# SSD decay factors: cumulative sums repeated over partitions from DRAM with a mask by GpSimd, instead of selector and mask matmuls

## The chip, the cores and the metric

The kernel runs on one core of a Trainium2 chip. The metric is the device time of one execution in microseconds (us). The engines are PE (TensorE, matmuls), DVE (VectorE) and ACT (ScalarE, elementwise work), POOL (GpSimd) and SP (which here issues DMAs). Each works through its own list of instructions in order; semaphores tie the lists together, so an instruction whose input isn't there holds up everything behind it on its engine.

## The reference

A trunk of two layers over 512 tokens of width 1024. Each layer is half a SwiGLU feed-forward block, a mixer, and another half block. The mixer of layer 0 is SSD (a selective state-space scan), that of layer 1 is S5. The change lies in SSD, whose scan goes over chunks of Q = 128 tokens; `bsz` is 1, there are 8 groups of 4 heads of 64 channels, with a state of 128:

```python
def step(state, inp):
    xc, dtc, bc, cc = inp
    cs = jnp.cumsum(dtc * A, axis=1)
    seg = cs[:, :, None] - cs[:, None]
    decay = jnp.exp(jnp.where(causal[None, :, :, None, None], seg, -jnp.inf))
    cb = jnp.einsum('btgn,bsgn->btsg', cc, bc)
    dtx = dtc[..., None] * xc
    y_diag = jnp.einsum('btsgk,bsgkp->btgkp', cb[..., None] * decay, dtx)
    y_off = jnp.einsum('btgn,bgkpn->btgkp', cc, state) * jnp.exp(cs)[..., None]
    to_end = jnp.exp(cs[:, -1:] - cs)
    new_state = (state * jnp.exp(cs[:, -1])[..., None, None]
                 + jnp.einsum('bsgn,bsgkp->bgkpn', bc, to_end[..., None] * dtx))
    return new_state, y_diag + y_off
```

Around it, `xs`, `bm` and `cm` come from projections of the normalised input, each followed by a causal convolution over 4 tokens and a silu; `z` comes from two gate projections for each group; the scan's output is gated by silu(z), normalised for each group and projected back.

## The kernel before

The stages follow each other: feed-forward (f1 of layer 0), SSD, f2, f1 of layer 1, S5, f2. Activations lie with channels on partitions and the 512 tokens along the row. Weights come by SP DMAs in blocks of 128 columns (`wst`, 4 buffers), are split into a rounded part `whi` (ACT, L213, 3 buffers) and a remainder `wlo` (DVE, L215), and a projection (`proj`, L222 to L224) is 24 matmuls of 128x512: high by high, low by high, high by low, for 8 blocks of the input.

In the SSD stage `dt` is projected first, `cs` (the cumulative sum, heads on partitions, tokens along the row) is made from it, and then the loop over groups g runs six projections: B, C, xs0, xs1 (each with `conv`: product with the input's scale L356, L358 and three L360, then `silu` L366), gate0 and gate1 (L390, L392). Between them, `pop()` sets in pieces of the scan of the group before, in this order: after B `states` and `decay(0)`, after C `outp(0)` and `decay(1)`, after xs0 `outp(1)`, after gate0 `norm`. After gate1 comes `head` of the group itself (L404 C by B into PSUM, copied by ACT as `cb` in L406; transposes of xs, L413, whose products with `dt` are L418; transposes of B, L424) and `final` of the group before (L160 spreads the group norm `nw_y` over partitions). For the first group, `head` stands behind the next group's B and every piece is one place later. After group 4 the first half of the output projection is made (8 blocks of 24 matmuls), with the pieces of scan 4 between them; at the end stand blocks of 12 matmuls, with the pieces of scan 7 between them.

`decay(e)` makes for the two heads h of half e the matrix of factors from token s (partition) to token t (row): PE copies row h of `cs` onto all partitions with a selector of ones (L454; `cshl` is `cs` split into two rounded parts), adds -1e30 above the diagonal (L455), ACT takes the exponential with -cs(s) as the bias (L459), and DVE multiplies by `cb` (L460). `outp(e)` likewise spreads `cs` over 64 partitions a head (L471) and takes its exponential (L473) as the factor of the state's part.

PE's order is the order of the program. The order on DVE, ACT, POOL and SP is set by a scheduler when the kernel is built. PSUM has two pools of 4 banks: `mm` for projections (and L471), `aux` for the rest: `head` takes four of `aux` for C by B, twice xs and B, so that L160 behind it takes the first again.

Of the kernel before, what the change touches and what calls it, by code (L numbers as in the profile page):

```python
# [30 lines left out]
def trunk_kernel(ctx, tc, x, ffn1_norm, ffn1_w_in, ffn1_w_out, mix_norm, ffn2_norm, ffn2_w_in, ffn2_w_out,  # L31
# [26 lines left out]

    ident = const.tile([128, 128], F32, name="ident")
    make_identity(nc, ident)  # L60
    identr = const.tile([128, 128], F32R, name="identr")
    ones = const.tile([128, 128], F32, name="ones")
    V.memset(ones, 1.0)
    kmask = const.tile([128, 16], F32, name="kmask")
# [2 lines left out]

    def masks():

        V.tensor_copy(identr, ident)  # L70
        V.tensor_reduce(kmask, ident.rearrange("p (k q) -> p k q", q=8), axis=AX.X, op=OP.add)
        V.tensor_reduce(qres, ident.rearrange("p (k q) -> p q k", q=8), axis=AX.X, op=OP.add)
        V.tensor_copy(qsel.rearrange("p (c q) -> p c q", q=8), qres[:, None, :].to_broadcast([128, 16, 8]))
# [51 lines left out]
    def both(*fs):  # L125
        return lambda: [f() for f in fs]
# [142 lines left out]
    def ssd(pr, nxt):  # L269
        w_in, w_out = ssd_in_proj[0], ssd_out_proj[0]  # L270
        with ExitStack() as es:
            sc = es.enter_context(tc.tile_pool(name="ssdc", bufs=1))
            sp = es.enter_context(tc.tile_pool(name="ssd", bufs=2))

            wd = wpool.tile([128, KD, 128], F32, name="wst", bufs=4)
            nc.sync.dma_start(wd[:, :, 0:32], w_in[:, 6144:6176].rearrange("(k p) c -> p k c", p=128))
            for q in range(1, 4):
# [3 lines left out]
            v = sp.tile([128, T], F32, name="y")  # L281
            V.tensor_tensor(v, pd, pr.rbc, op=OP.mult)
            V.tensor_scalar(v, v, col("dtb"), None, op0=OP.add)
            ax = sp.tile([128, T], F32, name="m")
            V.scalar_tensor_tensor(ax, v, -1.0, v, op0=OP.mult, op1=OP.max)
            ex = sp.tile([128, T], F32, name="m")
            S.activation(ex, ax, AF.Exp, scale=-1.0)
            w1 = sp.tile([128, T], F32, name="cv")
            V.tensor_scalar(w1, ex, 1.0, None, op0=OP.add)
            ln = sp.tile([128, T], F32, name="y")  # L290
            S.activation(ln, w1, AF.Ln)
            rw = sp.tile([128, T], F32, name="m")
            S.activation(rw, ln, AF.Exp, scale=-1.0)
            V.scalar_tensor_tensor(w1, w1, -1.0, ex, op0=OP.add, op1=OP.subtract)
            V.tensor_tensor(w1, w1, rw, op=OP.mult)
            dt = sp.tile([128, T], F32, name="m")
            V.scalar_tensor_tensor(dt, v, 0.0, ln, op0=OP.max, op1=OP.add)
            V.tensor_tensor(dt, dt, w1, op=OP.subtract)
            acol = sc.tile([128, 1], F32, name="acol")
# [12 lines left out]
            for c in range(4):  # L312
# [1 line left out]
                             bias=cse[:, c:c + 1])  # L314
            dce = sc.tile([128, 4], F32, name="dce")
            S.activation(dce, cse, AF.Exp)
            pack = sp.tile([128, T], F32, name="m")
            V.tensor_copy(pack[0:32], dt[0:32])
            V.tensor_scalar(pack[32:64], cs[32:64], -1.0, None, op0=OP.mult)
            V.tensor_tensor(pack[64:128], dt[64:128], ew[64:128], op=OP.mult)  # L320
            tok = sc.tile([128, 4, 128], F32, name="tok")
            cshl = sc.tile([128, T], F32R, name="cshl")
            S.copy(cshl, cs)
            V.tensor_tensor(cshl[32:64], cs[32:64], cshl[32:64].bitcast(F32), op=OP.subtract)
            sel = sc.tile([128, 32], F32R, name="sel")
            V.memset(sel.bitcast(F32), 0.0)
            V.tensor_copy(sel[0:32], ident[0:32, 0:32])
            V.tensor_copy(sel[32:64], ident[32:64, 32:64])
            mneg = sc.tile([128, 128], F32R, name="mneg")
            mf = sp.tile([128, 128], F32, name="mf", bufs=1)  # L330
            G.memset(mf, 0.0)
            G.affine_select(out=mf, in_=mf, compare_op=OP.is_ge, fill=-1e30, base=0, pattern=[[1, 128]],
                            channel_multiplier=-1)
            V.tensor_copy(mneg, mf)
# [60 lines left out]
            def scan(g, BT, CT, XS, SZ):  # L395
# [33 lines left out]
                def states():  # L429
# [15 lines left out]
                        SS[c + 1] = sn  # L445
                    st["SS"] = SS

                def decay(e):

                    M = []  # L450
                    for hh in range(2):
                        h = 4 * g + 2 * e + hh
                        pE = aux_ps()
                        PE.matmul(pE, sel[:, h:h + 1].to_broadcast([128, 128]), cshl, start=True, stop=False)  # L454
                        PE.matmul(pE, identr, mneg[:, None, :].to_broadcast([128, 4, 128]), start=False, stop=True)  # L455
                        m = sp.tile([128, T], F32, name="m")
                        for c in range(4):
                            s = slice(c * 128, (c + 1) * 128)
                            S.activation(m[:, s], pE[:, s], AF.Exp, bias=tok[:, c, 32 + h:33 + h])  # L459
                        V.tensor_tensor(m, m, st["cb"], op=OP.mult)  # L460
                        M.append(m)
                    st["M", e] = M

                def outp(e):
                    M = st["M", e]

                    selp = sp.tile([128, 2, 64], F32R, name="selp")
                    h0 = 4 * g + 2 * e
                    V.tensor_copy(selp, sel[:, h0:h0 + 2].bitcast(F32)[:, :, None].to_broadcast([128, 2, 64]))
                    pe_ = mm_ps()  # L470
                    PE.matmul(pe_, selp.rearrange("p a b -> p (a b)"), cshl, start=True, stop=True)  # L471
                    ecs = sp.tile([128, T], F32, name="ecs")
                    S.activation(ecs[:, 128:], pe_[:, 128:], AF.Exp)  # L473
                    po = aux_ps()
                    for c in range(1, 4):
                        s = slice(c * 128, (c + 1) * 128)
                        PE.matmul(po[:, s], st["SS"][c][:, e * 128:(e + 1) * 128], CT[:, s], start=True, stop=True)  # L477
                    V.tensor_tensor(ecs[:, 128:], ecs[:, 128:], po[:, 128:], op=OP.mult)
                    py = aux_ps()
                    for c in range(4):  # L480
                        for hh in range(2):
                            s = slice(c * 128, (c + 1) * 128)
                            k0 = (2 * e + hh) * 64
                            PE.matmul(py[hh * 64:(hh + 1) * 64, s], st["dtx"][:, c, k0:k0 + 64], M[hh][:, s], start=True,  # L484
                                      stop=True)
                    y = sp.tile([128, T], F32, name="y")
                    V.scalar_tensor_tensor(y, XS[e], col("sd", 2 * g + e), py, op0=OP.mult, op1=OP.add)
                    V.tensor_tensor(y[:, 128:], y[:, 128:], ecs[:, 128:], op=OP.add)
                    V.tensor_tensor(y, y, SZ[e], op=OP.mult)
                    sq = work.tile([128, T], F32, name="sq")  # L490
                    S.activation(sq, y, AF.Square)
                    st["y", e], st["sq", e] = y, sq
# [4 lines left out]
                def final():  # L497
                    pb = bcast_rows(st["r"])
                    for e in range(2):
# [5 lines left out]
                        V.tensor_tensor(yl, yn, yh.bitcast(F32), op=OP.subtract)  # L505
                        YH[2 * g + e], YL[2 * g + e] = yh, yl

                return both(head, *fin), [both(states, lambda: decay(0)), both(lambda: outp(0), lambda: decay(1)),
                                          lambda: outp(1), lambda: None, norm], final

            pend += [lambda: None] * 4 + [dt_tok]
# [668 lines left out]
```

## Time and profile before

| | us |
|---|---|
| median of 3 runs | 2107.82 (2107.75 to 2107.94) |
| the profiled execution | 2107.72 |
| its span | 2105.8 |

The span runs from the first to the last instruction; what lies around it is 1.92 us. PE is busy for 2054.7 us of it. The SSD stage's group loop lies about from 400 to 840 us. In the rows below a row begins with its start and its duration or its counts; "[0.80 <-DVE y L308]" is idle time before it and what ended it. Elementwise rows overlap a little at their ends with the next, and matmuls much more.

### The profile page before, as it was taken

What the parts mean: (1) busy time and instruction counts of PE and PEld (TensorE: products, weight loads), DVE (VectorE), ACT (ScalarE), POOL (GpSimd) and SP (SyncE); (2) the same over time, 40 slices, a digit from 0 to 9 for tenths busy, and PEclk for the clock granted to TensorE, in tenths of its full rate; (3) what the DMA queues carried; (4) which work ended last, traced back from release to release, by engine and by line L of the source; (5) the groups of instructions that cost most, each with busy time, mean ns of one, the idle gap of its engine ahead of it and who ended that gap; (6) DMA issues with size and microseconds to landing.
All of it is one profiled execution on the core that took longest, in us unless ns stands there. A gap on an engine that the chain in (4) does not pass through costs nothing.

```text
span 2105.8 us, 27114 instructions
## 1 busy us (share of the span) xinstructions
PE 2054.7 (98%) x10755; PEld 1691.9 (80%) x10755; DVE 1255.9 (60%) x2157; ACT 793.4 (38%) x1146; POOL 41.0 (2%) x114
## 2 busy tenths in 40 slices
PE   6999999999999999999999999999996999999997
PEld 5888888888888887887778888888886888888886
DVE  5698644687875788648864554344458555444444
ACT  4322322466663665333432333222344333222232
POOL 1000000000000000000000000000001000000000
PEclk8999999999999999999999999999997999999999
DMA  9355432322223213535553363333368233332331
GB/s 203 99 124 160 140 100 81 102 79 72 72 70 88 73 51 90 168 100 162 155 144 94 97 199 92 100 95 97 96 170 244 75 96 100 93 99 82 109 92 58
DMA packets 407630, 232.67 MB, mean 110 GB/s; under 512 B 44168, under 2 KB 395568, under 8 KB 407248
## 3 DMA queue, kind: packets, MB, share of 16 engines
q1 hardware_dynamic: 381152, 203.12, 34.1%
q10 hardware_dynamic: 22208, 13.91, 2.3%
q0 software_dynamic: 4144, 13.92, 2.0%
q8 instruction: 84, 1.38, 0.3%
q14 instruction: 42, 0.34, 0.0%
HBM read 206.21 MB, written 24.18 MB: 109 GB/s over the span
## 4 chain that ended last, share of the span: by engine, by line
PE 95%; DVE 3%; ACT 1%; DMA 1%; issue 1%; ACTq 0%; SPq 0%; DVEq 0%
PE mm L222 30%; PE mm L223 29%; PE mm L224 29%; PE aux L484 1%; PE aux L434 0%; PE aux L477 0%; PE aux L454 0%; PE aux L151 0%; PE aux L978 0%; DVE z L960 0%; PE aux L223 0%; PE aux L222 0%; PE aux L224 0%; PE aux L404 0%; PE aux L455 0%
## 5 line engine op out<-in xcount | busy, mean ns | idle before, releaser
L213 ACT CAST whi<-wst 128x1024 fp32r<-128x1024 f32 (+2 forms) x357 | 361.0, 1012 | 959.5 <-PE mm L223 660.5
L222 PE MATMUL mm<-hH,whi 128*128 128x512 f32 x1800 | 704.7, 392 | 3.2 <-DVE xT L1102 3.2
L223 PE MATMUL mm<-hL,whi 128*128 128x512 f32 x1800 | 702.8, 391 | 0.0
L224 PE MATMUL mm<-hH,wlo 128*128 128x512 f32 x1800 | 702.2, 390 | 0.0
L215 DVE TENSOR_TENSOR wlo<-wst,whi 128x1024 fp32r<-128x1024 f32 (+2 forms) x357 | 418.7, 1173 | 94.8 <-ACT whi L213 90.9
L222 PEld LDWEIGHTS mm<-hH,whi 128*128 128x128 f32 x1800 | 338.6, 188 | 75.0 <-ACT hH L1096 3.4
L224 PEld LDWEIGHTS mm<-hH,wlo 128*128 128x128 f32 x1800 | 338.6, 188 | 71.0 <-issue 0.6
L223 PEld LDWEIGHTS mm<-hL,whi 128*128 128x128 f32 x1800 | 338.6, 188 | 70.1 <-issue 0.6
L223 PE MATMUL mm<-al,whi 128*128 128x512 f32 x704 | 275.5, 392 | 0.0
L224 PE MATMUL mm<-ah,wlo 128*128 128x512 f32 x704 | 275.3, 392 | 0.0
L222 PE MATMUL mm<-ah,whi 128*128 128x512 f32 x704 | 274.7, 392 | 0.0
L248 DVE TENSOR_TENSOR up<-mm,rbc 128x512 f32<-128x512 f32 x88 | 60.7, 690 | 219.2 <-PE mm L224 219.0
L260 DVE SCALAR_TENSOR_TENSOR xT<-mm,xT 128x512 f32<-128x512 f32 x96 | 66.0, 689 | 194.7 <-PE mm L224 194.7
L223 PEld LDWEIGHTS mm<-al,whi 128*128 128x128 f32 x704 | 132.1, 188 | 29.0 <-issue 0.6
L222 PEld LDWEIGHTS mm<-ah,whi 128*128 128x128 f32 x704 | 132.1, 188 | 28.9 <-issue 0.6
L224 PEld LDWEIGHTS mm<-ah,wlo 128*128 128x128 f32 x704 | 132.1, 188 | 28.6 <-issue 0.2
L245 DVE TENSOR_TENSOR gt<-mm,rbc 128x512 f32<-128x512 f32 x88 | 60.7, 690 | 155.4 <-PE mm L224 150.3
L251 ACT CAST ah<-up 128x512 fp32r<-128x512 f32 x88 | 54.9, 623 | 60.2 <-DVE up L249 59.7
L360 DVE SCALAR_TENSOR_TENSOR cv<-raw,cols,cv 128x512 f32<-128x512 f32 x96 | 70.8, 744 | 0.7
L249 DVE TENSOR_TENSOR up<-up,gt 128x512 f32<-128x512 f32 x88 | 60.7, 690 | 11.0 <-ACT gt L246 4.4
L253 DVE TENSOR_TENSOR al<-up,ah 128x512 fp32r<-128x512 f32 x88 | 60.1, 683 | 1.2 <-ACT ah L251 1.0
L246 ACT ACTIVATE gt<-gt 128x512 f32<-128x512 f32 x88 | 55.2, 627 | 7.9 <-DMA d_P<-p_ks 4.2
(342 smaller groups left out, 1720.8 us busy)
## 6 DMA issues: line engine op xcount, KB each, us to landing
wst<-in_ffn_w_in_dram SPq DMA_DIRECT2D x176, 512.0 KB, 3.8
wst<-in_ffn_w_out_dram SPq DMA_DIRECT2D x64, 448.0 KB, 3.7
wst<-in_ssd_in_proj_dram SPq DMA_DIRECT2D x48, 512.0 KB, 3.9
wst<-in_ffn_w_out_dram SPq DMA_DIRECT2D x32, 512.0 KB, 4.0
opP<-d_P SPq DMA_DIRECT2D x16, 512.0 KB, 5.3
wst<-in_s_glu_w_dram POOLq DMA_DIRECT2D x12, 512.0 KB, 5.3
d_t<-p_cs POOLq DMA_DIRECT2D x8, 512.0 KB, 4.2
wst<-in_ssd_out_proj_dram SPq DMA_DIRECT2D x8, 512.0 KB, 4.1
```

Of the source, the lines that this page charges most:

```text
L213: S.copy(hi, st)
L215: V.tensor_tensor(lo, st, hi.bitcast(F32), op=OP.subtract)
L222: PE.matmul(ps, hi[:, k], H[k], start=first and k == 0, stop=False)
L223: PE.matmul(ps, hi[:, k], L[k], start=False, stop=False)
L224: PE.matmul(ps, lo[:, k], H[k], start=False, stop=last and k == n - 1)
L245: V.tensor_tensor(gt, pg, pr.rbc, op=OP.mult)
L246: S.activation(gt, gt, AF.Silu)
L248: V.tensor_tensor(up, pu, pr.rbc, op=OP.mult)
L249: V.tensor_tensor(up, up, gt, op=OP.mult)
L253: V.tensor_tensor(al, up, ah.bitcast(F32), op=OP.subtract)
L260: V.scalar_tensor_tensor(xT[d], po, 0.5, xT[d], op0=OP.mult, op1=OP.add)
L360: V.scalar_tensor_tensor(cv, raw[:, 1 + j:T + 1 + j], col("cw", j * 32 + ct), cv, op0=OP.mult, op1=OP.add)
```

## The change

`cs` (32 heads by 512 tokens) is stored to DRAM as `d_cs` by an SP DMA. For each half of a group, POOL's queue loads two rows of it onto all 128 partitions (`dec`, 512 KB) and columns 128 to 511 of each of the two onto 64 partitions (`ecs`, 96 KB each). POOL puts -1e30 above the diagonal of each chunk with an AFFINE_SELECT. ACT's exponentials then read and write SBUF in place, and one DVE product of 128x1024 takes the place of two of 128x512. L454, L455 and L471 are gone, and so are the copies `selp` and the set-up of selector and mask. `dec` has 2 buffers of two heads each, so a load waits until PE has read the matrices of the group before; an `ecs` load waits for DVE's sum in `outp` (L487 of the changed kernel).

```diff
-            ax = sp.tile([128, T], F32, name="m")
+            ax, ex = dec2()
...
-            cshl = sc.tile([128, T], F32R, name="cshl")
-            S.copy(cshl, cs)
-            V.tensor_tensor(cshl[32:64], cs[32:64], cshl[32:64].bitcast(F32), op=OP.subtract)
-            sel = sc.tile([128, 32], F32R, name="sel")
...
+            d_cs = dram.tile([32, T], F32, name="d_cs")
+            nc.sync.dma_start(d_cs, cs[0:32])
+
+            def cs_rows(dst, h, parts):
+                n = dst.shape[-1]
+                G.dma_start(dst, bass.AP(tensor=d_cs.tensor, offset=d_cs.offset + h * T + T - n,
+                                         ap=[[0, parts]] + [[T, k] for k in dst.shape[1:-1]] + [[1, n]]))
...
+                def rows(e):
+                    h = 4 * g + 2 * e
+                    m = sp.tile([128, 2, T], F32, name="dec")
+                    cs_rows(m, h, 128)
+                    ecs = sp.tile([128, T], F32, name="ecs")
+                    for hh in range(2):
+                        cs_rows(ecs[hh * 64:hh * 64 + 64, 128:], h + hh, 64)
+                    G.affine_select(out=m.rearrange("p h (c t) -> p (h c) t", c=4),
+                                    in_=m.rearrange("p h (c t) -> p (h c) t", c=4), compare_op=OP.is_ge, fill=-1e30,
+                                    base=0, pattern=[[0, 8], [1, 128]], channel_multiplier=-1)
+                    st["M", e], st["ecs", e] = m, ecs
+
                 def decay(e):
-                    M = []
+                    m = st["M", e]
                     for hh in range(2):
                         h = 4 * g + 2 * e + hh
-                        pE = aux_ps()
-                        PE.matmul(pE, sel[:, h:h + 1].to_broadcast([128, 128]), cshl, start=True, stop=False)
-                        PE.matmul(pE, identr, mneg[:, None, :].to_broadcast([128, 4, 128]), start=False, stop=True)
-                        m = sp.tile([128, T], F32, name="m")
                         for c in range(4):
                             s = slice(c * 128, (c + 1) * 128)
-                            S.activation(m[:, s], pE[:, s], AF.Exp, bias=tok[:, c, 32 + h:33 + h])
-                        V.tensor_tensor(m, m, st["cb"], op=OP.mult)
-                        M.append(m)
+                            S.activation(m[:, hh, s], m[:, hh, s], AF.Exp, bias=tok[:, c, 32 + h:33 + h])
+                    V.tensor_tensor(m, m, st["cb"][:, None, :].to_broadcast([128, 2, T]), op=OP.mult)
                 def outp(e):
-                    pe_ = mm_ps()
-                    PE.matmul(pe_, selp.rearrange("p a b -> p (a b)"), cshl, start=True, stop=True)
-                    ecs = sp.tile([128, T], F32, name="ecs")
-                    S.activation(ecs[:, 128:], pe_[:, 128:], AF.Exp)
+                    ecs = st["ecs", e]
+                    S.activation(ecs[:, 128:], ecs[:, 128:], AF.Exp)
...
-                return both(head, *fin), [both(states, lambda: decay(0)), both(lambda: outp(0), lambda: decay(1)),
+                rows(0)
+                return both(head, *fin, lambda: rows(1)), [both(states, lambda: decay(0)), both(lambda: outp(0), lambda: decay(1)),
```

Line numbers move a little: in the changed kernel L355 is the old L358, L357 the old L360, L363 the old silu L366, L389 the old L392, L403 the old L406, L415 the old L418, L441 the old L444, L476 the old L477; L472 is the exponential of `ecs`, L465 that of `dec`, L466 the product with `cb`, L490 the square in `outp`.

ACT's order moves in two places. The first is the first group. Before, from the cast of the first weights behind `cs` on (BT and CT are the silus of B and C, xs those of xs0 and xs1, TABLE_LOAD changes between the exponential's table and the silu's):

```order
L213 CAST whi<-wst 128x1024
L366 ACT_TABLE_LOAD
L366 ACTIVATE BT<-cv,cols_104 128x512
L366 ACTIVATE CT<-cv,cols_104 128x512
L213 CAST whi<-wst 128x1024
L358 ACTIVATE cv<-raw,cols_105 128x512 x2
L213 CAST whi<-wst 128x1024
L366 ACTIVATE xs_3479<-cv,cols_104 128x512
L366 ACTIVATE xs_3520<-cv,cols_104 128x512
```

With the change, from the first exponential of `ecs` on; behind the last of these rows come the silu of xs0, a load, seven more exponentials, a load, and the silu of xs1:

```order
L472 ACTIVATE ecs<-ecs 128x384
L363 ACT_TABLE_LOAD
L363 ACTIVATE BT<-cv,cols_103 128x512
L472 ACT_TABLE_LOAD
L472 ACTIVATE ecs<-ecs 128x384
L363 ACT_TABLE_LOAD
L363 ACTIVATE CT<-cv,cols_103 128x512
L355 ACTIVATE cv<-raw,cols_104 128x512 x2
L211 CAST whi<-wst 128x1024
L465 ACT_TABLE_LOAD
L465 ACTIVATE dec<-dec,tok 128x128 x9
L363 ACT_TABLE_LOAD
```

The exponentials of both halves stand ahead of the silus of xs0 and xs1, and those of `ecs` ahead of BT and CT, so each silu changes the table.

The second place is a group in the steady part, up to the copy `cb` of its head. Before (sq is the square of outp(1), sz the silus of the gates):

```order
L491 ACTIVATE sq<-y 128x512
L366 ACT_TABLE_LOAD
L366 ACTIVATE xs_5113<-cv,cols_104 128x512
L213 CAST whi<-wst 128x1024
L358 ACTIVATE cv<-raw,cols_105 128x512
L213 CAST whi<-wst 128x1024
L366 ACTIVATE xs_5180<-cv,cols_104 128x512
L392 ACTIVATE sz_5215<-cv 128x512
L213 CAST whi<-wst 128x1024
L392 ACTIVATE sz_5300<-cv 128x512
L406 COPY cb<-aux 128x512
```

With the change, of the same group (just ahead of these rows stand a load, an `ecs` exponential, six exponentials, an L355, two exponentials, the square of outp(1), a load and the silu of xs0):

```order
L211 CAST whi<-wst 128x1024
L465 ACT_TABLE_LOAD
L465 ACTIVATE dec<-dec,tok 128x128 x8
L472 ACTIVATE ecs<-ecs 128x384
L355 ACTIVATE cv<-raw,cols_104 128x512
L211 CAST whi<-wst 128x1024
L389 ACT_TABLE_LOAD
L389 ACTIVATE sz_5151<-cv 128x512
L363 ACTIVATE xs_5116<-cv,cols_103 128x512
L211 CAST whi<-wst 128x1024
L389 ACTIVATE sz_5236<-cv 128x512
L403 COPY cb<-aux 128x512
```

Eight exponentials, the `ecs` of the second half and two table loads have moved in ahead of `cb`; before, eight exponentials stood ahead of the group's CT and the other eight behind `cb`.

On DVE, behind the products L418 of the first group's head, from the first state on, before (L438, L440 and L444 are the states' chain, st the states):

```order
L438 COPY st_3717<-aux 128x256
L215 TENSOR_TENSOR wlo<-wst,whi 128x1024
L440 TENSOR_TENSOR st_3719<-st_3717,decS 128x256
L360 SCALAR_TENSOR_TENSOR cv<-raw,cols_105,cv 128x512
L444 TENSOR_TENSOR st_3719<-st_3719,aux 128x256
L460 TENSOR_TENSOR m<-m,cb 128x512
L360 SCALAR_TENSOR_TENSOR cv<-raw,cols_105,cv 128x512
L440 TENSOR_TENSOR st_3722<-st_3719,decS 128x256
L460 TENSOR_TENSOR m<-m,cb 128x512
L360 SCALAR_TENSOR_TENSOR cv<-raw,cols_105,cv 128x512
L444 TENSOR_TENSOR st_3722<-st_3722,aux 128x256
```

With the change, from the last two of those products on (behind these rows come an L357 and the last state's L437 and L441):

```order
L415 TENSOR_TENSOR wx<-aux,tok 128x256
L415 TENSOR_TENSOR dtx<-aux,tok 128x512
L466 TENSOR_TENSOR dec<-dec,cb 128x1024 x2
L357 SCALAR_TENSOR_TENSOR cv<-raw,cols_104,cv 128x512
L353 TENSOR_TENSOR raw<-mm,rbc 128x512
L357 SCALAR_TENSOR_TENSOR cv<-raw,cols_104,cv 128x512
L435 COPY st_3717<-aux 128x256
L213 TENSOR_TENSOR wlo<-wst,whi 128x1024
L357 SCALAR_TENSOR_TENSOR cv<-raw,cols_104,cv 128x512
L437 TENSOR_TENSOR st_3719<-st_3717,decS 128x256
L357 SCALAR_TENSOR_TENSOR cv<-raw,cols_104,cv 128x512
L441 TENSOR_TENSOR st_3719<-st_3719,aux 128x256
```

The products with `cb` stand together ahead of the chain of states, as two rows of 1024 columns; before, two of 512 columns stood within the chain.

## Rows read from the trace of the kernel before

**Rows 1.** The page's first part: busy time, share, instructions.
```profile
PE 2054.7 (98%) x10755; PEld 1691.9 (80%) x10755; DVE 1255.9 (60%) x2157; ACT 793.4 (38%) x1146; POOL 41.0 (2%) x114
```

**Rows 2.** What PE waited for, 380 to 860: total, times, longest.
```profile
PE aux L160 <- DVE nw_y L142: 0.9, 1, 0.9
PE aux L477 <- DVE st L444: 0.5, 1, 0.5
```

**Rows 3.** PE by line, 390 to 860: busy, mean ns, idle before.
```profile
L454 PE MATMUL aux<-cshl,sel 128*128 128x512 f32 x32 | 14.9, 467 | 0.0
```

**Rows 4.** Timeline of PE at the first `outp`: start, duration.
```profile
458.32 0.39 PE L471 MATMUL mm<-cshl,selp 128*128 128x512 f32 x1
458.55 0.83 PE L477 MATMUL aux<-CT,st 128*128 128x128 f32 x6
...
460.33 0.50 PE L454 MATMUL aux<-cshl,sel 128*128 128x512 f32 x1
```

**Rows 5.** Timeline of DVE around the first head.
```profile
444.14 1.23 DVE L215 TENSOR_TENSOR wlo<-wst,whi 128x1024 fp32r<-128x1024 f32 x1 [0.15 <-ACT whi L213]
445.28 0.68 DVE L418 TENSOR_TENSOR wx<-aux,tok 128x512 f32<-128x512 f32 x1
...
446.48 0.74 DVE L360 SCALAR_TENSOR_TENSOR cv<-raw,cols,cv 128x512 f32<-128x512 f32 x1
```

**Rows 6.** Timeline of ACT in a steady group.
```profile
549.82 1.28 ACT L366 ACT_TABLE_LOAD   x1
551.12 0.72 ACT L366 ACTIVATE CT<-cv,cols 128x512 f32<-128x512 f32 x1
...
554.09 0.49 ACT L473 ACTIVATE ecs<-mm 128x384 f32<-128x384 f32 x1
```

**Rows 7.** Timeline of ACT in the first group.
```profile
422.08 0.62 ACT L323 CAST cshl<-y 128x512 fp32r<-128x512 f32 x1 [0.80 <-DVE y L308]
423.28 1.28 ACT L313 ACTIVATE cv<-y,cse 128x128 f32<-128x128 f32 x4 [0.58 <-DVE cse L310]
...
426.01 1.03 ACT L213 CAST whi<-wst 128x1024 fp32r<-128x1024 f32 x1
...
438.58 1.34 ACT L366 ACTIVATE xs<-cv,cols 128x512 f32<-128x512 f32 x2
```

**Rows 8.** DMA issues of the whole span: count, size, median us to landing.
```profile
wst<-in_s_glu_w_dram POOLq DMA_DIRECT2D x12, 512.0 KB, 5.3
d_t<-p_cs POOLq DMA_DIRECT2D x8, 512.0 KB, 4.2
...
wst<-in_ssd_out_proj_dram SPq DMA_DIRECT2D x16, 256.0 KB, 2.7
```

**Rows 9.** Timeline of POOL: an issue, a mask, one copy made twice.
```profile
165.31 0.53 POOL L783 DMA_DIRECT2D d_t<-p_cs  x1 [7.23 <-DVE p_tb L561]
...
397.69 0.29 POOL L332 TENSOR_SCALAR_AFFINE_SELECT mf<-mf 128x128 f32<-128x128 f32 x1
...
1589.17 0.60 POOL L945 COPY rh<-rho 128x504 f32<-128x504 f32 x1
...
1597.67 1.08 POOL L945 COPY rh<-rho 128x504 f32<-128x504 f32 x1
```

**Rows 10.** Timeline of PE at the first head.
```profile
443.99 1.04 PE L413 MATMUL aux<-ident,xs 128*128 128x128 f32 x8
```

**Rows 11.** Timeline of all engines at a steady head.
```profile
567.01 0.15 DVE L135 TENSOR_SCALAR nw_v<-aux 128x4 f32<-128x4 f32 x1
...
569.18 1.06 PE L404 MATMUL aux<-CT,BT 128*128 128x128 f32 x8
...
569.45 0.69 DVE L390 TENSOR_TENSOR cv<-mm,rbc 128x512 f32<-128x512 f32 x1
...
570.72 0.57 ACT L406 COPY cb<-aux 128x512 f32<-128x512 f32 x1
...
571.34 0.65 PE L160 MATMUL aux<-ident,nw_y 128*128 128x128 f32 x4
```

More of the change, by code (lines that the diff above doesn't have):

```diff
@@ L60, in trunk_kernel @@
     make_identity(nc, ident)
-    identr = const.tile([128, 128], F32R, name="identr")
     ones = const.tile([128, 128], F32, name="ones")
@@ L68, in masks @@
     def masks():
-        V.tensor_copy(identr, ident)
         V.tensor_reduce(kmask, ident.rearrange("p (k q) -> p k q", q=8), axis=AX.X, op=OP.add)
@@ L273, in ssd, with dec2 @@
             sp = es.enter_context(tc.tile_pool(name="ssd", bufs=2))
+            def dec2():
+                m = sp.tile([128, 2, T], F32, name="dec")
+                return m[:, 0], m[:, 1]
             wd = wpool.tile([128, KD, 128], F32, name="wst", bufs=4)
@@ L283, in ssd @@
             V.tensor_scalar(v, v, col("dtb"), None, op0=OP.add)
-            ax = sp.tile([128, T], F32, name="m")
+            ax, ex = dec2()
             V.scalar_tensor_tensor(ax, v, -1.0, v, op0=OP.mult, op1=OP.max)
-            ex = sp.tile([128, T], F32, name="m")
             S.activation(ex, ax, AF.Exp, scale=-1.0)
@@ L291, in ssd @@
             S.activation(ln, w1, AF.Ln)
-            rw = sp.tile([128, T], F32, name="m")
+            rw, dt = dec2()
             S.activation(rw, ln, AF.Exp, scale=-1.0)
@@ L295, in ssd @@
             V.tensor_tensor(w1, w1, rw, op=OP.mult)
-            dt = sp.tile([128, T], F32, name="m")
             V.scalar_tensor_tensor(dt, v, 0.0, ln, op0=OP.max, op1=OP.add)
@@ L316, in ssd @@
             S.activation(dce, cse, AF.Exp)
-            pack = sp.tile([128, T], F32, name="m")
+            pack = dec2()[0]
             V.tensor_copy(pack[0:32], dt[0:32])
@@ L321, in ssd @@
             tok = sc.tile([128, 4, 128], F32, name="tok")
-            cshl = sc.tile([128, T], F32R, name="cshl")
-            S.copy(cshl, cs)
-            V.tensor_tensor(cshl[32:64], cs[32:64], cshl[32:64].bitcast(F32), op=OP.subtract)
-            sel = sc.tile([128, 32], F32R, name="sel")
[L326 to L334, printed above, removed]
+            d_cs = dram.tile([32, T], F32, name="d_cs")
[4 more added lines that the diff above has]
+                                         ap=[[0, parts]] + [[T, k] for k in dst.shape[1:-1]] + [[1, n]]))
             dd = sp.tile([32, 4, 32], F32, name="dd", bufs=1)
@@ L446, in states @@
                     st["SS"] = SS
+                def rows(e):
+                    h = 4 * g + 2 * e
+                    m = sp.tile([128, 2, T], F32, name="dec")
+                    cs_rows(m, h, 128)
[6 more added lines that the diff above has]
+                    st["M", e], st["ecs", e] = m, ecs
@@ L457, in decay @@
                         for c in range(4):
                             s = slice(c * 128, (c + 1) * 128)
-                            S.activation(m[:, s], pE[:, s], AF.Exp, bias=tok[:, c, 32 + h:33 + h])
-                        V.tensor_tensor(m, m, st["cb"], op=OP.mult)
-                        M.append(m)
-                    st["M", e] = M
+                            S.activation(m[:, hh, s], m[:, hh, s], AF.Exp, bias=tok[:, c, 32 + h:33 + h])
+                    V.tensor_tensor(m, m, st["cb"][:, None, :].to_broadcast([128, 2, T]), op=OP.mult)
@@ L464, in outp @@
                 def outp(e):
                     M = st["M", e]
-                    selp = sp.tile([128, 2, 64], F32R, name="selp")
-                    h0 = 4 * g + 2 * e
-                    V.tensor_copy(selp, sel[:, h0:h0 + 2].bitcast(F32)[:, :, None].to_broadcast([128, 2, 64]))
-                    pe_ = mm_ps()
-                    PE.matmul(pe_, selp.rearrange("p a b -> p (a b)"), cshl, start=True, stop=True)
-                    ecs = sp.tile([128, T], F32, name="ecs")
-                    S.activation(ecs[:, 128:], pe_[:, 128:], AF.Exp)
+                    ecs = st["ecs", e]
@@ L483, in outp @@
                             k0 = (2 * e + hh) * 64
-                            PE.matmul(py[hh * 64:(hh + 1) * 64, s], st["dtx"][:, c, k0:k0 + 64], M[hh][:, s], start=True,
+                            PE.matmul(py[hh * 64:(hh + 1) * 64, s], st["dtx"][:, c, k0:k0 + 64], M[:, hh, s], start=True,
                                       stop=True)
```

## The prediction

> **What bounds the kernel now.** I read the page's list of engines first: PE is busy for 98% of the span [rows 1], so time can only leave where PE has less to do, and comes back wherever PE starts to wait. Next the list of what PE waits for in the SSD stage. Its two entries that matter here are 0.9 us, once, for `nw_y`, and 0.5 us, once, for the state `st` [rows 2]. A shorter PE program therefore finds engines that are only just in time, and the question is how much of the removed work each of them lets through.
>
> **What goes from PE.** The rows grouped by line have 32 matmuls of L454 at a mean of 467 ns [rows 3]; their partners in L455 are as many, and `outp` has one of L471 in each of its 16 calls: 80 matmuls of 512 columns. Their cost is not the duration, since they overlap: L471 starts at 458.32 and L477 behind it at 458.55 [rows 4], a pitch of 0.23 us. The long mean of L454 is in the first of a pair, behind a float32 matmul; that change of type stays, for the projection that follows then. 80 x 0.23 = 18.4 us, 2.3 us for each of 8 groups. The small set-up casts and the 16 `selp` copies on DVE lie in slack and are counted at nothing.
>
> **What the new pieces take.** Two elementwise rows overlap at their ends: wlo, listed at 1.23, is followed 1.14 later [rows 5], so I take 0.09 off each elementwise row: 0.59 for a product of 512 columns, 0.65 for an L360, 1.14 for a product of 1024 in SBUF (wlo is the nearest). On ACT: table load 1.30 to the next start, silu 0.63 and the convolution's first product L358 the same, `ecs` exponential 0.40 [rows 6], cast 1.03, an exponential of 128 columns from SBUF (1.28 - 0.09) / 4 = 0.30 [rows 7]. A POOL DMA of 512 KB lands in 4.2 to 5.3 us, an SP DMA of 256 KB in 2.7 [rows 8]; I use 2.7 for the small ones too. Issue costs POOL 0.53. The mask over 128x128 took 0.29, so 128x1024 takes at most 8 x 0.29 = 2.3; at the rate of L945's copy (504 columns in 0.60) it takes 1.2 [rows 9]. So rows that are free to be loaded at 0 are ready at 0.5 + 4.2 + 1.2 = 5.9 to 0.5 + 5.3 + 2.3 = 8.1.
>
> **The first group.** `cs` is ready where the old cast of it starts, 422.08 [rows 7]. Stored (2.7), it is in DRAM at 424.8. SP's next weight issue is not held up, since it comes later. POOL then issues four `ecs` loads (to 426.9), the first pair landing at 425.3 + 2.7 = 428.0, and the two big loads with a mask behind each. The mask of the first ends at 426.9 + 0.5 + 4.2 + 2.3 = 433.9; the second load is issued only behind it, so its mask ends at 433.9 + 0.5 + 4.2 + 2.3 = 440.9. ACT's order now has `ecs` exp, load, BT, load, `ecs` exp, load, CT, two L355, cast, load, nine exponentials, load, xs0, load, seven exponentials, load, xs1. From 428.0: 428.4, 429.7, 430.3, 431.6, 432.0, 433.3, 433.9, 435.2, 436.2, 437.5, eight exponentials 439.9, the ninth waits for the second mask (440.9) to 441.2, 442.5, 443.1, 444.4, 446.5, 447.8, 448.4. Today both silus begin at 438.58 in one block [rows 7], and the transposes that read xs1 are on PE at 443.99 [rows 10]. PE waits 448.4 - 444.0 = 4.4 us. Ends: 3.4 when the near mask price holds (the ninth exponential is then in time), 6.6 when loads take 5.3 (both masks are then 1.1 later). Behind it, DVE has the two 1.14 us products straight after the head's L415s, where before two of 0.59 stood ahead of the last state: 2.28 - 1.18 = 1.1 later, while PE comes to L477 earlier by five matmuls, 1.15. L477 already waits 0.5 [rows 2], so all 2.2 are added. First group: +6.6.
>
> **Groups 2, 3, 4, 6 and 7.** Here ACT's order decides. The bank that L160 writes is freed by ACT's copy `cb`, which stands last in the queue. Now `cb` starts at 570.72 and L160 at 571.34 [rows 11], with 0.05 to spare. After the change twice eight exponentials (0.30 each) and two more table loads stand between outp(0) and `cb`, where the old row of eight had gone by before. I count from the end of projection xs0, with the lines of the changed kernel (L355 is the old L358, L357 the old L360, and so on, three lower). ACT: cast to 1.0, load 2.3, `ecs` 2.7, six exponentials 4.5, L355 5.1, two exponentials 5.7; the square of outp(1) needs y and ends 6.9; load 8.2, silu xs0 8.8, cast 9.8, load 11.1, eight exponentials 13.5, `ecs` 13.9, L355 of xs1 14.5. DVE then: first L357 15.2, z 15.8, second L357 16.4, wlo 17.5, one Newton step 17.7, third L357 18.4, the rest of the Newton chain (567.01 to 569.45 is the whole of it, 2.4 [rows 11]) 20.6, second z 21.2. ACT: second sz 21.8, `cb` 22.4 and its handover 22.5. PE: outp(1) from 458.55 to 460.33 is 1.78 [rows 4], a projection of 24 matmuls at 0.23 is 5.5; 1.8 + 5.5 + 5.5 + 0.65 + 5.5 + 2.15 (head up to L160, 569.18 to 571.34 [rows 11]) = 21.1. The difference is 1.4; some twenty handovers between engines are in the chain and none in the sum, and I take 2.0, with 0 and 3 as ends. So 2.0 of the 2.3 come back in each of four groups: +8.0 (the fifth, group 7, is in the tail).
>
> Are the rows in time? The first buffer is free at the end of outp(0), 5.5 before the zero above, its exponentials' turn is at 2.7: 8.2 after the release against 5.9 to 8.1. The second is free at the end of outp(1), 1.8; ready 7.7 to 9.9, turn 11.1. In time, the first by 0.1 in the worst case. The halo memsets of `raw` that stand behind the mask in POOL's queue are covered by several us of projection; if the cover went, conv would start late.
>
> **The tail and group 4.** In the last scan the projection slots are of 12 matmuls, half as long, and the state chain stands behind the two products: I give its 2.3 back entirely (ends 0 and 4). Scan 4 lies among the long slots of the out projection with no convs beside it: its 2.3 are kept.
>
> Sum: -18.4 + 6.6 + 8.0 + 2.3 = -1.5. The profiled execution took 2107.72 against a span of 2105.8 (the table above); its time is 0.1 from the median 2107.82. 2107.7 - 1.5 = 2106.2.
>
> **A rule weighed.** Two equal L945 copies took 0.60 and 1.08 [rows 9]: something shared stretches POOL's work by 1.8. The Trainium skill, SBUF — State Buffer, section "SBUF: two separate sides", calls the port pair of GpSimd and DVE an exclusive lock: a GpSimd operation that reads SBUF and a DVE operation with two SBUF inputs block each other for the whole instruction. By that rule the masks (and DVE's many two-input operations beside them) lengthen each other, which is the third rival below. By row 0.60 alone the masks are in time; by row 1.08 they aren't.
>
> **Rivals.**
> R1, steady waits are hidden (chance 0.20): the 2.0 hangs on a sum of 22 us with small links; if ACT's casts or the square come earlier, `cb` is in time. For it: `cb` is just in time today; against: two more loads and eight more exponentials certainly stand ahead. 2107.7 - 18.4 + 6.6 + 2.3 = 2098.2.
> R2, everything is hidden (0.08): 2107.7 - 18.4 = 2089.3. Against: the first group's row of table loads cannot start before 424.8.
> R3, the rows come late (0.30), the one on the slower side. Place: the first exponential of each group, in ACT's in-order queue, waits for load and mask, and all that stands behind it, `cb` too. If the mask is stretched as L945 was, 2.3 x 1.8 = 4.1, rows are ready at 9.9, 1.7 beyond the turn at 8.2; five groups and the first group's two masks in series pay it: 5 x 1.7 + 2 x 1.8 = +12, 2118. It decides from 8.2 us of load and mask onward; a load that reads 128 times the same DRAM row slower than 5.3 us does the same.
> The forecast, delays about equal to the gain, 0.42; its own range 2103.5 to 2112.
>
> **How the numbers follow.** 0.2% (4.2 us) is about what a measurement of this kernel can tell from no change: 2103.6 to 2112.0. Faster: R1 and R2, 0.28. Same: 0.42. Slower: R3, 0.30. The range from 2097 to 2119 leaves out R2 and about a third of R3.
>
> **What would show it.** With the changed kernel's lines: L160 waits for `cb` about 2 us in groups 2, 3, 4, 6, 7; L410 waits about 4.4 once for xs1; L476 about 2.7 once for `st`; PE has 80 matmuls fewer and no other new wait. Masks at 1.2 to 2.3 us, loads at 4.2 to 5.3. If ACT's exponentials wait for AFFINE_SELECT in every group, R3 is right; if PE's list of waits stays as short as now, R2. The prediction is wrong most easily in the 2.0, which stands for several small links times four.

## The result

| | us, median | lowest to highest |
|---|---|---|
| before, 4 runs | 2107.88 | 2107.75 to 2108.36 |
| the change, 4 runs | 2123.53 | 2121.0 to 2130.29 |

The ratio is 1.0078, with a 95% interval from 1.0065 to 1.009: slower by 15.7 us, where 2106.2 and a range of 2097 to 2119 had been forecast. The profiled execution took 2122.07 with a span of 2119.3. The stretch from the SSD stage's first sum of squares on PE (L151 before, L149 after) to its last L160 (L158 after) took 462.0 us before and 476.4 after, +14.4, so nearly all of it is in that stage; it is called "the stage" below. Its first and last rows, before and then with the change:

```profile
400.70 0.44 PE L151 MATMUL aux<-ones,sq 128*32 128x1 f32 x32
...
862.74 0.60 PE L160 MATMUL aux<-ident,nw_y 128*128 128x128 f32 x4
```

```profile
399.86 0.44 PE L149 MATMUL aux<-ones,sq 128*32 128x1 f32 x32
...
876.24 0.60 PE L158 MATMUL aux<-ident,nw_y 128*128 128x128 f32 x4
```

The first part of the page of the changed kernel answers to [rows 1]:

```profile
PE 2044.9 (96%) x10675; PEld 1681.2 (79%) x10675; DVE 1252.0 (59%) x2119; ACT 786.2 (37%) x1137; POOL 84.2 (4%) x176
```

80 matmuls are gone, POOL alone got busier, by 43 us, and still the span grew. PE must wait more. What PE waited for from 380 to 880 (total, times, longest), against [rows 2]:

```profile
PE aux L410 <- ACT xs L363: 12.8, 6, 5.2
PE aux L158 <- ACT cb L403: 9.7, 6, 1.8
PE aux L476 <- DVE st L441: 2.8, 3, 2.0
PE aux L158 <- DVE nw_y L140: 0.9, 1, 0.9
PE aux L149 <- ACT sq L490: 0.7, 1, 0.7
```

26.9 us, where it was 2.4: the two rows of [rows 2] and this one.

```profile
PE aux L151 <- ACT sq L491: 1.0, 1, 1.0
```

Of the five rows with the change the first two are the places that the forecast named; in groups 2, 3, 4 and 6 there are two waits in each head, not one. PE's timeline at the head of group 2:

```profile
532.32 0.27 PE L410 MATMUL aux<-ident,xs 128*128 128x128 f32 x1
534.03 0.98 PE L410 MATMUL aux<-ident,xs 128*128 128x128 f32 x7 [1.44 <-ACT xs L363]
534.85 0.49 PE L421 MATMUL aux<-ident,BT 128*128 128x128 f32 x3
537.14 1.11 PE L158 MATMUL aux<-ident,nw_y 128*128 128x128 f32 x4 [1.80 <-ACT cb L403]
...
538.48 0.63 PE L221 MATMUL mm<-hL,whi 128*128 128x512 f32 x1
538.91 0.63 PE L222 MATMUL mm<-hH,wlo 128*128 128x512 f32 x1
```

PE waits 1.44 us for the silu of xs1 and 1.80 for `cb`. Behind that the same matmuls start every 0.43 us and not every 0.23. The mean granted clock (the number ahead of the DMA share) in stretches around the first head and the heads of groups 2, 3 and 4:

```profile
440.00:460.00 20.00, 12.85 (x58) 10.80 (x58) 11.93 (x17) 15.98 (x30) 0.20 (x2) 0.83 0.30 80
...
530.00:545.00 15.00, 11.76 (x57) 9.76 (x57) 12.87 (x29) 6.47 (x10) 0.10 (x1) 0.89 0.25 70
545.00:620.00 75.00, 71.53 (x500) 58.73 (x500) 55.45 (x92) 45.13 (x78) 11.60 (x23) 1.00 0.39 107
620.00:635.00 15.00, 11.79 (x57) 9.65 (x55) 13.67 (x29) 8.04 (x12) 0.10 (x1) 0.89 0.28 81
```

At three of the stops the clock fell to its lower level (1.2 of 2.4 GHz) and stayed there for a few us after PE went on. The head of group 3 (at 578) had the same two waits, 1.67 and 1.81, and stayed at 1.00. From L158 to the first fast matmul took 2.91 us in group 2 where the same six rows took 1.64 in group 3; the three stretches, worked out so, cost some 1.7 + 1.3 + 1.5 = 4.5 us.

Where the waits come from is in the chain of waits of group 3. ACT's rows in it, from its timeline:

```profile
561.73 1.28 ACT L472 ACT_TABLE_LOAD   x1 [2.14 <-DMA ecs<-d_cs]
...
563.45 1.85 ACT L465 ACTIVATE dec<-dec,tok 128x128 f32<-128x128 f32 x6
...
571.03 1.28 ACT L465 ACT_TABLE_LOAD   x1
572.33 2.45 ACT L465 ACTIVATE dec<-dec,tok 128x128 f32<-128x128 f32 x8
...
579.82 0.72 ACT L363 ACTIVATE xs<-cv,cols 128x512 f32<-128x512 f32 x1 [1.13 <-DVE cv L357]
...
582.56 0.63 ACT L389 ACTIVATE sz<-cv 128x512 f32<-128x512 f32 x1 [1.08 <-DVE cv L387]
583.10 0.57 ACT L403 COPY cb<-aux 128x512 f32<-128x512 f32 x1
```

Ahead of these the chain has a landing of 5.3 us for `ecs` (556.33 to 561.66), issued once DVE had freed its buffer. Then ACT does its block of exponentials, a table load, the block of the second half, and only then, with two short waits for DVE, xs1 and `cb`. In the first group ACT's queue is the one that the forecast had written down, some 2 us later:

```profile
428.71 0.53 ACT L472 ACTIVATE ecs<-ecs 128x384 f32<-128x384 f32 x1 [2.79 <-DMA ecs<-d_cs]
...
439.23 1.28 ACT L465 ACT_TABLE_LOAD   x1 [1.92 <-issue]
440.52 2.75 ACT L465 ACTIVATE dec<-dec,tok 128x128 f32<-128x128 f32 x9
...
448.78 1.28 ACT L363 ACT_TABLE_LOAD   x1
450.08 0.72 ACT L363 ACTIVATE xs<-cv,cols 128x512 f32<-128x512 f32 x1
```

The issues that answer to [rows 8], and the masks (count, total, mean):

```profile
dec<-d_cs POOLq DMA_DIRECT2D x16, 512.0 KB, 4.4
...
ecs<-d_cs POOLq DMA_DIRECT2D x32, 96.0 KB, 4.5
```

```profile
L453 POOL TENSOR_SCALAR_AFFINE_SELECT dec<-dec 128x1024 f32<-128x1024 f32 x16 | 18.1, 1133 | 21.2 <-DMA dec<-d_cs 21.2
```

`dec` and its mask kept to their bounds (4.4 us, 1.13 us). `ecs`, a fifth as large, needed 4.5 and not 2.7.

### The profile page after: what moved, and what is told of

Read it like the earlier page. It is cut to its first block, busy times and chain, and to the rows that moved or that the text cites. A ratio compares the mean times of both kernels' runs of the same rounds, so it can differ in the third digit from the quotient of the medians.

```text
span 2119.3 us, 27043 instructions
## 1 busy us (share of the span) xinstructions
PE 2044.9 (96%) x10675; PEld 1681.2 (79%) x10675; DVE 1252.0 (59%) x2119; ACT 786.2 (37%) x1137; POOL 84.2 (4%) x176
## 4 chain that ended last, share of the span: by engine, by line
PE 66%; DVE 6%; ACT 4%; issue 2%; DMA 1%; POOL 0%; ACTq 0%; DVEq 0%
PE mm L220 21%; PE mm L221 21%; PE mm L222 21%; ACT dec L465 1%; DVE cv L357 1%; DMA ecs<-d_cs 1%; DVE wlo L213 1%; ACT whi L211 0%; DVE z L960 0%; PE aux L431 0%; ACT L465 0%; PE aux L222 0%; PE aux L220 0%; PE aux L221 0%; PE aux L821 0%
## 5 line engine op out<-in xcount | busy, mean ns | idle before, releaser
L357 DVE SCALAR_TENSOR_TENSOR cv<-raw,cols,cv 128x512 f32<-128x512 f32 x96 | 72.6, 762 | 36.8 <-ACT cv L355 36.3
```

The source lines that it names most:

```text
L357: V.scalar_tensor_tensor(cv, raw[:, 1 + j:T + 1 + j], col("cw", j * 32 + ct), cv, op0=OP.mult, op1=OP.add)
```

## The experiments

Each ran beside the kernel before (medians 2108.2 to 2108.6); the change did not run again, so a difference from its 2123.53 lies between medians of separate measurements, in which the kernel before differs by up to 0.8. Three theories were carried: T, ACT's order makes the waits; U, the rows land too late; V, POOL's masks and the row DMAs slow others wherever they stand. "Stage" is the stretch defined above, in the profiled execution.

| | median us | ratio, 95% interval | stage us |
|---|---|---|---|
| 1 all exponentials behind cb | 2095.64 | 0.9938 (0.9924 to 0.9953) | 448.1 |
| 2 the same, first group alone | 2116.15 | 1.0039 (1.0026 to 1.0051) | 467.7 |
| 3 four ecs buffers | 2122.70 | 1.0067 (1.0052 to 1.0082) | 476.0 |
| 4 no table loads | 2097.40 | 0.9949 (0.9934 to 0.9964) | 452.1 |
| 5 ecs exponentials behind cb | 2111.84 | 1.0016 (1.0007 to 1.0026) | 468.7 |
| 6 dec by rows alone | 2122.57 | 1.0067 (1.0052 to 1.0082) | 474.9 |
| 7 ecs by rows alone | 2105.64 | 0.9986 (0.9977 to 0.9996) | 459.9 |
| 8 behind cb, and yh in group 4 | 2088.08 | 0.9903 (0.9888 to 0.9917) | 443.4 |
| 9 dec exponentials behind cb | 2105.02 | 0.998 (0.9971 to 0.999) | 457.3 |
| 10 experiment 8, masks twice | 2089.32 | 0.9909 (0.9893 to 0.9926) | 444.2 |

**1. All exponentials behind cb.** The scheduler is made to put them there by data:

```diff
                     S.copy(st["cb"], pcb)
+                    nb = sp.tile([128, 4, 4], F32, name="nb")
+                    V.scalar_tensor_tensor(nb, st["cb"][:, 0:16].rearrange("p (c h) -> p c h", c=4), 0.0,
+                                           tok[:, :, 32 + 4 * g:36 + 4 * g], op0=OP.mult, op1=OP.add)
+                    zb = sp.tile([128, 1], F32, name="zb")
+                    V.tensor_scalar(zb, st["cb"][:, 0:1], 0.0, None, op0=OP.mult)
...
-                            S.activation(m[:, hh, s], m[:, hh, s], AF.Exp, bias=tok[:, c, 32 + h:33 + h])
+                            S.activation(m[:, hh, s], m[:, hh, s], AF.Exp, bias=st["nb"][:, c, 2 * e + hh:2 * e + hh + 1])
...
-                    S.activation(ecs[:, 128:], ecs[:, 128:], AF.Exp)
+                    S.activation(ecs[:, 128:], ecs[:, 128:], AF.Exp, bias=st["zb"])
```

> All loads, masks and matmuls of the changed kernel stay; both kinds of exponential get a bias that is made from cb (cb times 0, plus the old bias), so that ACT can only do them behind the copy cb of the same group. Theory T (ACT's order: exponentials and table loads stand ahead of the xs1 silu and of cb, PE waits for both at each head, and its clock falls after the longer waits): waits of the heads on xs1 and cb go from 22.5 us to under 3, the time to 2089 to 2097. Theory U (the rows themselves come too late for their use): the rows are used later here, so the same 2089 to 2097, this run does not part it from T. Theory V (POOL's masks and the row DMAs slow the other engines wherever they stand): most of the loss stays, 2110 or more.

2095.64: 27.9 us less than the change, with the same loads, masks and matmuls. The longest of PE's waits in the stage:

```profile
PE mm L220 <- ACT yh L509: 2.3, 1, 2.3
```

The three others (`nw_y`, `st`, the square) add up to 1.9; no wait for xs1 or `cb` is left. V falls as the cause: POOL's work and the transfers are all there. T stands; U isn't told apart. The new order also needs fewer table loads (see 4), so this run shows order and loads together.

**2. The first group alone.** The two biases of experiment 1 where `g == 0`, the old ones elsewhere.

> The same tie of the exponentials to cb, for group 0 alone. T: the first group's waits on xs1 (7.2 us, two pieces) and the slow clock behind them (about 1.7) go, some 9 us: 2112 to 2116. U and V speak of rows and masks in all groups: 2119 to 2125, no clear gain.

2116.15, 7.4 us less than the change, just above the 2112 to 2116 that T gave. All waits for xs1 are gone, the first group's 7.2 us and also the 5.7 of groups 2, 3, 4 and 6, where no bias was changed; one wait for `cb` grew to 4.1 us and one for the square to 3.2. So the run agrees with T, but does not give the first group's share by itself.

**3. Four ecs buffers.**

```diff
-                    ecs = sp.tile([128, T], F32, name="ecs")
+                    ecs = sp.tile([128, T], F32, name="ecs", bufs=4)
```

> Four buffers instead of two for the ecs rows, so their loads need not wait for DVE's sum in outp; ACT's order nearly as in the changed kernel. U: ACT starts its block of exponentials as soon as the first dec rows are masked, the waits at the steady heads (about 3.1 us a group in 5 groups) mostly go with their slow clock: 2100 to 2106. T: the block starts 1 to 2 us earlier in a group, of 3.1 us of waits some 1 to 2 stay: 2112 to 2119. V: no gain, 2121 to 2125.

2122.70, as the change; the interval of its ratio overlaps. That is V's figure, though V had fallen with experiment 1; T (2112 to 2119) and U (2100 to 2106) were both missed. It was not the experiment I meant. With a buffer free sooner, the program loads `ecs` a group sooner, and the scheduler takes its exponential a group sooner too (four of them now stand in the first group), behind the same landing. ACT's timeline in it:

```profile
560.15 1.28 ACT L472 ACT_TABLE_LOAD   x1 [1.81 <-DMA ecs<-d_cs]
```

So the run says nothing on U, and little on T.

**4. No table loads.** Both kinds of exponential give only the bias here, through a function that needs no load; the decay's values are left out.

```diff
-S.activation(m[:, hh, s], m[:, hh, s], AF.Exp, bias=tok[:, c, 32 + h:33 + h])
+S.activation(m[:, hh, s], m[:, hh, s], AF.Identity, scale=0.0, bias=tok[:, c, 32 + h:33 + h])
...
-S.activation(ecs[:, 128:], ecs[:, 128:], AF.Exp)
+S.activation(ecs[:, 128:], ecs[:, 128:], AF.Identity, scale=0.0)
```

> Both exponentials are replaced by a pass of the same size that yields the bias alone (a function that every table holds), so the values are not the reference's; ACT's order is the same row for row without 32 table loads. T: every load is 1.3 us in ACT's queue ahead of xs1 and cb, three or four a steady group and six in the first: all steady waits go and the first group keeps under 1 us: 2090 to 2097. U: rows are as late as before, 2116 to 2122. V: unchanged, 2121 to 2125.

2097.40, 0.4 above what T gave. ACT's order is otherwise the same row for row, the rows land as late (4.5 us for `ecs`) and ACT waits 0.6 to 1.5 us for them in four groups, yet of PE's waits at the heads 0.7 us are left (the largest other is for the state chain):

```profile
PE aux L476 <- DVE st L441: 3.9, 4, 2.1
...
PE aux L158 <- ACT cb L403: 0.7, 1, 0.7
```

U as the sole cause falls (2116 to 2122 was its figure): a queue that is shorter by the loads takes late rows without a wait on PE. It is not that the change has more loads. Before, ACT made 40 in the stage's exponentials and silus, the change makes 33, experiment 1 makes 16; first before, then the change (count, total, mean):

```profile
L366 ACT ACT_TABLE_LOAD x20 | 25.7, 1283 | 0.4
L473 ACT ACT_TABLE_LOAD x12 | 15.4, 1283 | 0.2
L459 ACT ACT_TABLE_LOAD x8 | 10.3, 1283 | 0.1
```

```profile
L363 ACT ACT_TABLE_LOAD x11 | 14.1, 1283 | 0.2
L472 ACT ACT_TABLE_LOAD x9 | 11.5, 1283 | 5.0 <-DMA ecs<-d_cs 4.8
L465 ACT ACT_TABLE_LOAD x7 | 9.0, 1283 | 2.0 <-issue 1.9
L389 ACT ACT_TABLE_LOAD x6 | 7.7, 1283 | 0.1
```

Experiment 9 below has 42 and is 18.5 us faster than the change. What the change has is loads and exponentials that stand ahead of xs1 and `cb` of a head instead of behind them.

**5 and 9. Half of the tie.** Experiment 1 with the bias of `zb` alone (5) or of `nb` alone (9).

> Of the tie to cb only the half on ecs: ACT takes the ecs exponentials behind cb, the dec exponentials and their table loads stay ahead of xs1 and cb. T: the block starts at the end of the mask and not at the landing of ecs (1.0 to 2.1 us later in the changed kernel) and is 0.9 us shorter, but the loads stay: 1 to 2 us of the 3.1 us stay at a steady head, the first group keeps about 3 of 7: 2104 to 2113. If the late ecs rows alone made the waits (U): steady waits under 0.5 us, 2100 or less.

> The other half of the tie: the dec exponentials go behind cb, the ecs exponentials stay where the change puts them, each with its loads, waiting for its row. With both early 2123.5, ecs alone late 2111.8, both late 2095.6. T with dec and ecs as costs that add up would give 2123.5 - (28 - 12) = 2107; T with one queue in which the first 10 us of lateness are hidden and the rest is paid in full gives less, 2098 to 2104. U (late ecs rows as the cause): 2112 or more.

Experiment 5 lies where T put it (2104 to 2113) and not where U did (2100 or less). Against the change, moving the `ecs` exponentials takes off 11.7 us, moving the `dec` exponentials 18.5, both 27.9: nearly a sum (30.2), so little of one half is hidden behind the other; of the two figures for 9 by T, 2107 with a sum and 2098 to 2104 without, 2105.02 lies between. In experiment 5 the waits for `cb` stay, those for xs1 fall to 2.6 us:

```profile
PE aux L158 <- ACT cb L403: 9.3, 6, 1.8
```

In experiment 9 ACT waits 10.2 us in all for `ecs` rows and PE only 0.6 for `cb`: late rows alone make hardly any wait at the heads. How much of the 11.7 is the late landing of `ecs` and how much its exponentials and their loads, these two runs don't part.

**6 and 7. One part of the change alone.** 6 keeps `cshl`, `sel` and L471 and drops the `ecs` loads; 7 keeps L454, L455 and the mask on PE and adds the `d_cs` store and the `ecs` loads.

> dec by rows and mask as in the change, ecs by the selector matmul and PSUM as before: 16 matmuls (3.7 us) are back on PE. T: 16 exponentials and their loads stand ahead of xs1 and cb all the same, about 2 to 3 us a head and the slow clock: 2115 to 2124. U with the late ecs rows as the cause: the heads wait no more, 2096 to 2102 (3.7 more than without the selector).

> ecs by rows as in the change, the decay by selector and mask matmuls as before: only 16 matmuls (3.7 us) are gone, no mask on POOL. T: the dec exponentials stay behind cb, but each ecs exponential has a load of its own and waits for its row: one or two loads more ahead of xs1 and cb, 0 to 2 us a group: 2104 to 2115. U: the rows of ecs land as late as in the change and hold ACT's queue: 2112 to 2120.

The decay's part alone is as slow as the whole (2122.57, where U gave 2096 to 2102); its longest stop is 5.2 us for `cb`. ACT waits for no row in the group loop of this kernel, since `ecs` comes from PSUM, yet PE stands still at the heads of groups 2, 3, 4 and 6 for about 0.58 (xs1) and 1.8 (`cb`):

```profile
PE aux L158 <- ACT cb L410: 12.8, 6, 5.2
...
PE aux L417 <- ACT xs L370: 4.8, 5, 2.5
```

So 2.4 us a head come from the queue without late rows, and the change's heads wait 2.9 to 3.5. The part on `ecs` alone, at 2105.64 within T's 2104 to 2115, gains 2.6 us of the 3.7 that leave PE: its `ecs` lands in 2.6 us, with no `dec` load ahead of it in POOL's queue, and PE waits 2.2 us in all for `cb`:

```profile
PE aux L160 <- ACT cb L414: 2.2, 4, 0.6
```

**8. The best version.** In experiment 1 PE waited 2.3 us for `yh` of group 3 at the start of the output projection, since ACT does that cast among the exponentials. For group 4 the biases are made from the last `yh`:

```diff
+                    if g != 4:
+                        tie(st["cb"])
...
-                return both(head, *fin, lambda: rows(1)), [both(states, ...
+                return both(head, *fin, lambda: rows(1), *([lambda: tie(YH[7].bitcast(F32))] if g == 4 else [])), [both(states, ...
```

> The first experiment, and in group 4 the exponentials wait for the last cast yh of group 3 instead of cb, since PE waited 2.3 us there for yh at the start of the out projection. T: 2.3 us off the first experiment, 2092 to 2095; if another engine is late next there, the same as it, 2095.6.

2088.08, ratio 0.9903 (0.9888 to 0.9917): 20.1 us below the kernel before, and below what I expected. PE's waits in the stage are these and one of 0.2:

```profile
PE aux L158 <- DVE nw_y L140: 0.9, 1, 0.9
PE aux L486 <- DVE st L451: 0.7, 1, 0.7
```

The stage took 443.4, 18.7 less than before: the forecast's 18.4, with 0.6 us less of waits than before. Of the 7.6 us by which the median lies below experiment 1, 4.7 are in the stage: 2.3 are that wait, and the granted clock behind it, 0.98 from 545 to 620 there and 1.00 here, is some 1.5 us. Where the rest comes from is not shown.

**10. Masks twice.** Experiment 8 with each AFFINE_SELECT a second time.

> The eighth experiment with every mask put on twice (the second changes nothing): 16 more operations of 1.1 us on POOL. T: rows have slack there, so 0 to 1 us more than 2088.1, from collisions with DVE. V (POOL's work slows DVE wherever it stands, about 0.9 us for each mask that meets a DVE operation): 3 us more or above, 2091 to 2100.

2089.32: 1.2 us more for 16 masks, just over T's 0 to 1. The intervals of the two ratios overlap, so these 1.2 are not clear of the noise; the highest of the four runs, 2089.8, is below V's 2091. The masks took 1.3 and 1.4 us on average there, against 1.1 in the change, and PE, ACT and DVE waited for none.

## Why the prediction was wrong, point by point

**What leaves PE: right.** 18.4 us were worked out; experiment 8, where PE's waits are 0.6 shorter than before and its matmuls otherwise the same, shows 18.7 in the stage.

**The first group: the right place, too small.** 4.4 us of wait for xs1 were forecast, 1.98 + 5.17 = 7.15 came. The queue was the right one. It ended at 450.8 and not 448.4. No exponential waited for a mask: the second was over at 436.7. But ACT began the block at 439.23, where I had 436.2. The profile names no releaser for that wait ("issue"); by its time it was the bias `tok`, a copy that DVE does behind three L357 of the group's convolutions, which themselves wait for ACT:

```profile
435.79 2.77 DVE L357 SCALAR_TENSOR_TENSOR cv<-raw,cols,cv 128x512 f32<-128x512 f32 x3 [5.29 <-ACT cv L355]
438.48 0.68 DVE L341 COPY tok<-aux 128x512 f32<-128x512 f32 x1
```

The copy ended at 439.16; I had not asked when `tok` is there. The mask had a small part in it: it ran from 435.60 to 436.69, and the first of the three L357 took 1.44 beside it, where others take 0.74.

Behind the head 2.2 us for the state's chain were forecast; L476 there waited 0.36. The 2.2 rested on a misreading: the 0.5 of [rows 2] was taken for a wait of the first group, but it stands in the tail of the kernel before, and the first group's L477 had not waited:

```profile
800.25 0.49 PE L477 MATMUL aux<-CT,st 128*128 128x128 f32 x2 [0.51 <-DVE st L444]
```

So 6.6 for the first group against 7.15 + 0.36 = 7.5 is near in part by luck: xs1 was forecast too short, and the chain behind it too long.

**Groups 2, 3, 4, 6 and 7: the step that failed.** The sum gave 1.4, I took 2.0 with 3 as the end. The heads of groups 2, 3, 4 and 6 waited 1.44 + 1.80, 1.67 + 1.81, 1.41 + 1.80 and 1.13 + 1.80: 12.9 us, where 8.0 were forecast; group 1, which I had counted at nothing, added 1.3 and group 7 1.2. The mechanism was right, exponentials and loads ahead of `cb` in ACT's queue; what failed is a term of the sum, the landing of `ecs`. I had reckoned only whether `dec` and its mask are in time for their turn, and they were (mask over at 559.1 in group 3, turn at 561.7). The small `ecs` load was put at 2.7 us from an SP row of [rows 8]; in POOL's queue, issued behind the 512 KB of `dec`, it took 4.5 (median) and up to 5.6, and ACT, whose first row of the block it feeds, waited 1.0, 2.1, 1.0 and 0.7 us for it in groups 2, 3, 4 and 6. The sum's 1.4 with this wait added makes 2.4, 3.5, 2.4 and 2.1; measured were 3.2, 3.5, 3.2 and 2.9, so the small links are worth up to 0.8 a group, where 0.6 were taken. Experiment 6, where no row lands late (it also has L471 back on PE), has 2.4 a head, not far from the forecast's 2.0; by it the landing made some 3.4 of the 4.9 us that the four heads lacked. So the third rival, rows late for their turn, came about by a load that it did not name, and in these groups the mask, on which it rested, was in time.

The forecast followed the queue to `cb` alone. The silu of xs1 stands in it too, and PE's L410 needs it ahead of L158, so the delay shows in two stops. By the forecast's own times (third L357 at 18.4, head from about 19) xs1 would have been there, so this by itself adds nothing to the sum.

**The clock: a term put at nothing.** Some 4.5 us in the profiled execution. The waits and the clock make -18.7 + (26.9 - 2.4) + 4.5 = +10.3 of the stage's 14.4. The other 4 are not accounted for; a part lies in pitches at the stops (a first L410 cut off from its seven others takes 0.27 where it has 0.11 in a row). The four runs lay from 2121.0 to 2130.3 with mean clocks of 0.979 to 0.986, the slowest at the lowest.

**The tail: right.** 2.3 were forecast, L476 waited 2.02 + 0.42 there for the state chain behind the two products, where 0.5 had been waited before; group 7's 1.2 for `cb` comes on top.

**The rule weighed.** Its mechanism is in the trace. POOL's and DVE's timelines of the changed kernel at one mask:

```profile
518.94 1.31 POOL L453 TENSOR_SCALAR_AFFINE_SELECT dec<-dec 128x1024 f32<-128x1024 f32 x1 [1.56 <-DMA dec<-d_cs]
```

```profile
518.55 0.75 DVE L357 SCALAR_TENSOR_TENSOR cv<-raw,cols,cv 128x512 f32<-128x512 f32 x1 [2.51 <-ACT cv L355]
519.22 1.58 DVE L488 TENSOR_TENSOR y<-y,sz 128x512 f32<-128x512 f32 x1
```

L488 is 0.69 long elsewhere; here it ends at 520.80, so 0.69 us of work would have begun at 520.1, near the mask's end at 520.25; and the mask, 1.09 alone, is longer by about the time for which L357 still ran. That agrees with the Trainium skill, SBUF — State Buffer, section "SBUF: two separate sides", on the lock between GpSimd and DVE. A DVE row that reads one input from PSUM, at 658.59, took its usual 0.69 inside a mask. Five of the 16 masks met a DVE operation in this way: three times L488 grew by 0.9 us, twice an L357 by 0.7 and 0.8. In group 3, where none did, the waits at the head were no shorter (1.67 and 1.81 against 1.44 and 1.80).

The chances said 0.30 for slower; the range ended 4.5 us too low.

## What to carry to other kernels

When work moves from the engine that bounds to one that looks idle, its place in that engine's in-order queue is the price: here exponentials that the scheduler took early (presumably because their rows are there early; no run tests the reason) stood with their table loads ahead of a copy and a silu for which PE waits, and 16 us were lost with the same row loads, masks and matmuls that gain 20 once the exponentials stand behind that copy. Follow such a queue to every row that the bounding engine reads, not to the last alone. A false dependence (a bias made from 0 times the tile to be waited for) set the order in experiments 1 and 8 at the price of two small DVE operations a group.

## What the runs showed of the hardware

Two heads with nearly the same waits (1.44 + 1.80 and 1.67 + 1.81 us) left the granted clock at its lower level for some 3 us in one case and untouched in the other. A DMA of 96 KB from POOL's queue took 4.5 us (median) in the change and 2.6 in experiment 7, which has no loads of 512 KB in that queue. In experiment 1, with all the loads, those issued behind a 512 KB load that had landed took 2.5 to 2.8 in 13 of 14 cases, those issued while it was under way 4.2 (median of 14); four that were issued ahead of the first large one took 4.4 to 5.1. An activation-table load took 1.28 us every time, and in 37 of 43 cases the next row of ACT began 1.29 us after its start. The mask over 128x1024 took 1.09 us undisturbed, under a half of eight times the 0.29 of the 128x128 one in [rows 9].
